# A hybrid encoder trunk on one core: one slot pitch, a fused mask with paired blocks in FoX, and another order in the head

## The chip, the cores and the metric

The kernel runs on one core of a Trainium2 chip. The metric is device time in microseconds (us). TensorE (PE) multiplies, VectorE (DVE) and ScalarE (ACT) work elementwise, GpSimd (POOL) does a little, and SyncE (SP) issues the DMAs.

## The reference

Two layers over x (512 tokens, 1024 features), all fp32. Layer 0 mixes by a chunkwise mLSTM, layer 1 by forgetting attention (FoX) with 16 heads of 64; each is followed by a squared-ReLU MLP of width 4096. Each sub-layer normalises x, scales and shifts it by vectors that come from the condition c, and adds its gated output to x.

```python
mod = silu(c) @ ada_w[l] + ada_b[l]
sh1, sc1, g1, sh2, sc2, g2 = split(mod, 6)
h = rms_norm(x) * (1 + sc1) + sh1
x = x + g1 * mixer(h)                 # mLSTM (l = 0) or FoX (l = 1)
h = rms_norm(x) * (1 + sc2) + sh2
x = x + g2 * (square(relu(h @ w1)) @ w2)
# FoX, per head, for s <= t:
logit[t, s] = q_t . k_s / sqrt(64) + F_t - F_s
out = softmax(where(s <= t, logit, -inf)) @ v
```

## The kernel before, in words

Activations lie transposed, features on partitions, as eight tiles of 128x512. To keep fp32 accuracy every large product is done three times with operands split in a high and a low part (`prod3`, lines 296 to 298, and `gemm_b`, lines 361 to 363): hi·lo, lo·hi, hi·hi. A `unit` (line 138) loads 512 KB of weights and splits them: ACT casts the high part `whi`, DVE subtracts the low part `wlo`.

The tiles of activations come from one pool, `gp`. Slots of tag "g" (40 of them) are 516 columns wide, since the mLSTM's v tiles carry two more columns per head (ones in the high part, zeros in the low); in the built program they start 2,080 bytes apart. Slots of the tags "kt" and "qt" (8 each) are 512 columns wide and start 2,048 bytes apart, and so do the halves of the weight tiles. The MLP's hidden tiles `uh`, `ul` lie in "kt" and "qt" for the chunks c = 0 and 2 and in "g" for c = 1 and 3; h lies in "g", the input of the K and V products (`kvh`, `kvl`) in "kt" and "qt".

**The head.** SP loads a first group `u` of conditioning weights (2 MB), then x (2 MB), a unit of w_in and further groups. PE computes the rows of the conditioning for a group (`ada_rows_first`, line 172: four at a time, each on 32 columns of the array), ACT copies them out, PE transposes them (line 158), and DVE makes shift and scale from them (lines 178 to 181). The mean square of x (squares on ACT, line 250, sums on DVE, line 254, a product with ones on PE, line 262) gives 1/rms by Ln and Exp on ACT (264, 265). `modulated` (285, 287, 288) makes h from it, and the q product runs over k with four banks of PSUM, tag "A". The conditioning rows, their transposes and the mean square share the one bank of tag "C". Then follow the gates and the key product, which takes "A" again, and the v product, "A" too.

**FoX** (from line 565) runs over 8 pairs of heads and 4 query blocks. In a step PE computes the logits of the step after next (686, 687; then `maskb` times `identb` in bf16 adds -1e30 above the diagonal, 688), transposes the probabilities of this step (710), multiplies those of the step before with V (`weighted`, 727), and does two rounds of the q product of a later pair (`FILL`). DVE takes the row maximum (697), ACT the exponential with its row sum (699), DVE the reciprocal and the scaling (700, 701) and half the copies of the transposes (715), ACT the other half (713).

PE, ACT, DVE and SP each take their instructions in order. Where nothing is pinned, a scheduler in the framework places them; in the head the source pins PE's order.

## Time and profile before

| | us |
|---|---|
| median of 3 runs (1242.35 to 1243.93) | 1243.78 |
| the profiled execution's own time | 1243.87 |
| its span | 1241.8 |
| PE busy | 1212.4 (98%) |
| DVE busy | 715.0 (58%) |
| ACT busy | 486.5 (39%) |
| first product of the q projection starts | 27.82 |

A span row gives busy time of matmuls whose ends are modelled and overlap; what a product costs is read from one start to the next. In the timeline a row has start, length, engine, line, operation, output<-inputs, shapes, count, and in brackets the idle time before it and what ended it. In the windows a row has the window, its length, busy us and count of PE, PEld (weight loads), DVE, ACT and POOL, then the granted clock, the DMA engines' share and GB/s. In the groups a row ends with busy us, mean ns of one, and the idle time before.

### The profile page before, as it was taken

The page shows a single profiled execution, that of the slowest core. Times are in us where ns is not written, and L with a number is a line of the kernel's source. Part 1 is how long each engine was busy: PE and PEld are TensorE (multiplying, and loading weights), DVE is VectorE, ACT ScalarE, POOL GpSimd, SP SyncE. Part 2 cuts the span into 40 slices and gives each one's busy share as a digit, 9 for nine tenths or more (in the row PEclk, how much of TensorE's full clock was granted, in tenths as well). Part 3 has the DMA queues.
Part 4 walks back from the last instruction along what each step waited for, and adds up shares of the span by engine and source line. Part 5 has one row for each costly group of instructions (what it writes and reads, how often), then busy time and mean ns, then how long its engine had stood idle before and what let it go on. Part 6 is the DMA issues. An engine that isn't in the chain of part 4 may idle for free.

```text
span 1241.8 us, 16417 instructions
## 1 busy us (share of the span) xinstructions
PE 1212.4 (98%) x6262; PEld 990.3 (80%) x6262; DVE 715.0 (58%) x1193; ACT 486.5 (39%) x876; POOL 56.9 (5%) x78
## 2 busy tenths in 40 slices
PE   4999999999999999999999999999999999999997
PEld 1677888897887888788988877779988888888886
DVE  3687568797656664575565467764843443333344
ACT  3443664264123233133445456643632332332343
POOL 0001001100000000000100111101000000000001
PEclk9999999999999999999999999999999999999999
DMA  9666215546644663565143354422332323323312
GB/s 337 237 206 194 86 51 178 177 138 203 216 158 144 205 193 102 169 209 165 35 122 99 116 144 104 111 58 68 106 105 95 102 88 99 97 91 102 91 46 68
DMA packets 66255, 165.01 MB, mean 133 GB/s; under 512 B 9537, under 2 KB 11841, under 8 KB 66177
## 3 DMA queue, kind: packets, MB, share of 16 engines
q1 hardware_dynamic: 65088, 162.92, 42.1%
q8 instruction: 49, 0.80, 0.3%
q10 hardware_dynamic: 1088, 1.05, 0.3%
q14 instruction: 30, 0.24, 0.1%
HBM read 153.39 MB, written 2.10 MB: 125 GB/s over the span
## 4 chain that ended last, share of the span: by engine, by line
PE 91%; DVE 4%; DMA 3%; ACT 1%; issue 1%; SPq 0%; DVEq 0%; ACTq 0%
PE ga L296 22%; PE ga L298 22%; PE ga L297 22%; PE gb L361 4%; PE gb L363 3%; PE gb L362 3%; DMA araw<-in_adaw_dram 2%; PE oT L727 2%; PE q L651 2%; PE pT L710 1%; PE q L652 1%; PE q L653 1%; PE lg L686 1%; DVE wlo L138 1%; PE lg L687 1%; PE ada L172 1%
## 5 line engine op out<-in xcount | busy, mean ns | idle before, releaser
L138 DVE TENSOR_TENSOR wlo<-raw,whi 128x1024 fp32r<-128x1024 f32 x192 | 236.3, 1231 | 270.0 <-ACT whi L137 268.7
L137 ACT CAST whi<-raw 128x1024 fp32r<-128x1024 f32 x192 | 201.1, 1049 | 454.5 <-PE ga L298 367.0
L296 PE MATMUL ga<-hl,whi 128*128 128x512 f32 (+1 forms) x640 | 238.7, 373 | 1.0 <-DVE hl L288 1.0
L298 PE MATMUL ga<-hh,whi 128*128 128x512 f32 (+1 forms) x640 | 238.0, 372 | 0.0
L297 PE MATMUL ga<-hh,wlo 128*128 128x512 f32 (+1 forms) x640 | 237.8, 372 | 0.0
L296 PE MATMUL ga<-ul,whi 128*128 128x512 f32 (+1 forms) x576 | 211.6, 367 | 0.0
L297 PE MATMUL ga<-uh,wlo 128*128 128x512 f32 (+1 forms) x576 | 211.4, 367 | 0.0
L298 PE MATMUL ga<-uh,whi 128*128 128x512 f32 (+1 forms) x576 | 211.3, 367 | 0.0
L202 DVE SCALAR_TENSOR_TENSOR adaacc<-araw,cond,adaacc 128x512 f32<-128x512 f32 x140 | 106.0, 757 | 73.6 <-DMA araw<-in_adaw_dram 72.2
L296 PEld LDWEIGHTS ga<-hl,whi 128*128 128x128 f32 x640 | 120.5, 188 | 28.6 <-DVE hl L288 3.9
L298 PEld LDWEIGHTS ga<-hh,whi 128*128 128x128 f32 x640 | 120.4, 188 | 22.4
L297 PEld LDWEIGHTS ga<-hh,wlo 128*128 128x128 f32 x640 | 120.4, 188 | 22.4
L296 PEld LDWEIGHTS ga<-ul,whi 128*128 128x128 f32 x576 | 108.3, 188 | 19.5 <-issue 0.8
L298 PEld LDWEIGHTS ga<-uh,whi 128*128 128x128 f32 x576 | 108.2, 188 | 19.3 <-issue 0.8
L297 PEld LDWEIGHTS ga<-uh,wlo 128*128 128x128 f32 x576 | 108.3, 188 | 18.5
L784 DVE SCALAR_TENSOR_TENSOR x<-ga,mod,x 128x512 f32<-128x512 f32 (+1 forms) x72 | 46.0, 688 | 29.4 <-PE ga L298 29.4
L770 DVE TENSOR_TENSOR r<-r 128x512 f32<-128x512 f32 (+1 forms) x72 | 44.2, 626 | 17.8 <-ACT r L769 17.8
L254 POOL TENSOR_TENSOR sq<-sq,sq 128x512 f32<-128x512 f32 x12 | 17.8, 1481 | 790.7 <-ACT sq L250 790.3
L769 ACT ACTIVATE r<-ga 128x512 f32<-128x512 f32 (+1 forms) x72 | 38.6, 547 | 38.3 <-PE ga L298 37.7
L361 PE MATMUL gb<-wlo,hh 128*128 128x512 f32 x128 | 51.1, 401 | 0.8 <-DVE kl L138 0.8
L362 PE MATMUL gb<-whi,hl 128*128 128x512 f32 x128 | 50.6, 396 | 0.0
L363 PE MATMUL gb<-whi,hh 128*128 128x512 f32 x128 | 50.4, 395 | 0.0
(199 smaller groups left out, 1695.2 us busy)
## 6 DMA issues: line engine op xcount, KB each, us to landing
raw<-in_w_dram SPq DMA_DIRECT2D x128, 512.0 KB, 3.6
araw<-in_adaw_dram SPq DMA_DIRECT2D x160, 256.0 KB, 3.4
raw<-in_win_dram SPq DMA_DIRECT2D x24, 512.0 KB, 4.0
u<-in_adaw_dram SPq DMA_DIRECT2D x32, 256.0 KB, 5.9
raw<-in_wkv_dram SPq DMA_DIRECT2D x16, 512.0 KB, 3.6
raw<-in_woa_dram SPq DMA_DIRECT2D x8, 512.0 KB, 3.5
raw<-in_wq_dram SPq DMA_DIRECT2D x8, 512.0 KB, 3.6
q<-qh SPq DMA_DIRECT2D x32, 128.0 KB, 2.3
```

The source lines that it names most:

```text
L137: nc.scalar.copy(dst_hi, src)
L138: dve.tensor_tensor(dst_lo, src, dst_hi.bitcast(F32), op=ALU.subtract)
L202: stt(acc[g], u, cond[:, k:k + 1], acc[g], op0=ALU.mult, op1=ALU.add)
L296: put(mm(ps[:, sl], wh[:, kk, c], rlo[k][:, sl], start=k == 0, stop=False))
L297: put(mm(ps[:, sl], wl[:, kk, c], rhi[k][:, sl], start=False, stop=False))
L298: put(mm(ps[:, sl], wh[:, kk, c], rhi[k][:, sl], start=False, stop=k == NJ - 1))
L361: mm(ps[t], lhi[k][:, c], wl[:, kk], start=k == 0, stop=False)
L362: mm(ps[t], llo[k][:, c], wh[:, kk], start=False, stop=False)
L363: mm(ps[t], lhi[k][:, c], wh[:, kk], start=False, stop=k == NJ - 1)
L769: act(r, ps[:, sl], AF.Relu)
L770: dve.tensor_tensor(r, r, r, op=ALU.mult)
L784: stt(xt[j][:, sl], ps[:, sl], modc(l, G2, j), xt[j][:, sl], op0=ALU.mult, op1=ALU.add)
```

## The change

**Pitch.** All slots of `gp` are 512 columns wide. The high parts of v get a pool of their own (`vp`, four tiles of 516), the low parts lose their two columns of zeros (the product with them writes 256 columns instead of 258). A pad of 128 bytes stands ahead of `gp`; in the built program every slot of `gp` then starts at the same place modulo 2,048 bytes, and as far from the weight tiles, modulo 2,048, as "kt" and "qt" did before. "g" has 37 slots instead of 40.

**FoX.** q and its bias row are negated, so the logits come out negated. The bf16 mask product goes; a DVE instruction adds a mask (0 or 1e30) to the logits out of PSUM, writes the sum to SBUF and its row minimum beside it; ACT takes the exponential from SBUF. The transposes of two query blocks are put side by side, and `weighted` runs once for two query blocks, with 256 columns where both need the key block.

**Head.** x is loaded first, then the unit of w_in, then the first conditioning group in two halves of 128 columns each for shift and scale. The mean square stands first on PE. The second conditioning group's rows come after the q products of k = 0 and 1. Twelve products of the key projection (k = 0, 1; m = 0, 1, banks "B") are done between the conditioning groups, and the key projection uses "BBAA".

```diff
-GSLOT = 2 * (DV + 2)
+VW = 2 * (DV + 2)
...
-    gp = ctx.enter_context(tc.tile_pool(name="gp", bufs=40))
+    vp = ctx.enter_context(tc.tile_pool(name="vp", bufs=NT))
+    pad = ctx.enter_context(tc.tile_pool(name="pad", bufs=1))
+    gp = ctx.enter_context(tc.tile_pool(name="gp", bufs=37))
+    pad.tile([P, 32], F32, name="pad")
...
-                mm(ps[:, ts], identb, maskb, start=False, stop=True)
...
-                dve.tensor_reduce(mx, ps[:, :n], axis=AX.X, op=ALU.max, negate=True)
-                act(p, ps[:, :n], AF.Exp, bias=mx, accum_out=dn)
+                dve.tensor_tensor_reduce(p, LG[a, i][:, :n], mask[:, S - n:], 1.0, POS, ALU.add, ALU.min, mx)
+                act(p, p, AF.Exp, bias=mx, scale=-1.0, accum_out=dn)
...
+                for jp, t in enumerate(PT[pr, i // 2, a]):
+                    js = slice(2 * jp, min(2 * jp + 2, i + 1))
+                    src = tp[:, js.start * P:js.stop * P].rearrange("p (j q) -> p j q", q=P)
...
+                    mm(oT[64 * a:64 * a + 64, (i - 1) * P + q0:(i + 1) * P], V[j, h // 8][:, c:c + DH], PT[pr, i // 2, a][j // 2][:, j % 2, q0:],
...
-            if n:
+            if n and not i % 2:
                 weighted(*steps[n - 1])
...
+    uq = [unit(win[0, 0])]
+    u = ada_load(0, HALF)
+    r0 = rstd(FULL, [squares(range(6), FULL), squares((6, 7), FULL)], put=pin)
+    rows = [ada_rows_first(u[0])]
+    ada_first(0, rows[0])
+    modulated(0, SH1, 0, r0, FULL, hhi, hlo, js=(0,))
+    rows = ada_rows_first(u[1])
+    ada_first(1, rows)
+    modulated(0, SH1, 0, r0, FULL, hhi, hlo, js=(1,))
+    u, = ada_load(1)
+    qproj0(0)
+    qproj0(1)
+    kpre = {"us": [unit(win[1, 0])], "ps": {m: bank("ga", "B") for m in range(2)}, "k": 2}
```

The order of PE at the program's start, before: `ada` are conditioning rows, `adaT` their transposes, `ms` the mean square, `ga` the q product.

```order
L172 MATMUL ada_164<-u_143,condb_98 32x512
...
L158 MATMUL adaT_175<-ident,adarow_173 128x128 x4
L262 MATMUL ms_206<-sq_184,ones_d 128x512
L262 MATMUL ms_206<-sq_204,ones_d 128x512
L172 MATMUL ada_246<-u_233,condb_98 32x512
...
L172 MATMUL ada_246<-u_236,condb_98 32x512
L296 MATMUL ga_212<-hl_132,whi_219 128x512
```

PE at the same place, now (lines 268, 174, 183 and 302 are the old 262, 172, 158 and 296):

```order
L268 MATMUL ms_200<-sq_178,ones_d 128x512
L268 MATMUL ms_200<-sq_195,ones_d 128x512
L174 MATMUL ada_210<-u_157,condb_105 32x256
...
L183 MATMUL adaT_221<-ident,adarow_219 128x128 x2
L174 MATMUL ada_232<-u_157,condb_105 32x256
...
L183 MATMUL adaT_243<-ident,adarow_241 128x128 x2
L302 MATMUL ga_206<-hl_132,whi_151 128x512
```

The mean square has moved to the front, the first group's rows stand in two halves, and the second group's rows (`ada_246` before) are behind the products of k = 0 and 1.

PE where the key product (`ga_557`, `ga_558`) ends and the v product (`gb`) starts, before:

```order
L298 MATMUL ga_557<-hh_131,whi_671 128x512
L296 MATMUL ga_558<-hl_139,whi_671 128x512
L297 MATMUL ga_558<-hh_131,wlo_670 128x512
L298 MATMUL ga_558<-hh_131,whi_671 128x512
L361 MATMUL gb_720<-wlo_726,hh_124 128x512
```

And now, with the first key products (`ga_300`, `ga_301`) right behind the second conditioning group (`ada_302`):

```order
L174 MATMUL ada_302<-u_260,condb_105 32x512
L302 MATMUL ga_300<-hl_132,whi_297 128x512
...
L302 MATMUL ga_301<-hl_132,whi_297 128x512
...
L183 MATMUL adaT_319<-ident,adarow_311 128x128 x4
L302 MATMUL ga_300<-hl_133,whi_297 128x512
...
L304 MATMUL ga_600<-hh_131,whi_689 128x512
L367 MATMUL gb_738<-wlo_744,hh_124 128x512
```

The last key products now fill the two "A" banks that were taken last, and `gb_738` starts in one that the key product did not use.

PE in one step of FoX, from the logits `lg` of block 1 on (`pT` transposes, `oT` V products), before:

```order
L686 MATMUL lg_6830<-k_1317_6612,q_1332_6670 128x256
L687 MATMUL lg_6830<-k_1179_6118,q_1183_6122 128x256
L688 LDWEIGHTS identb
L688 MATMUL lg_6830<-maskb,identb 128x128
L686 MATMUL lg_6834<-k_1334_6678,q_1333_6674 128x256
L687 MATMUL lg_6834<-k_1180_6119,q_1184_6123 128x256
...
L710 MATMUL pT_6852<-ident,p_6791 128x128 x4
L710 MATMUL pT_6859<-ident,p_6798 128x128 x4
L727 MATMUL oT_6771<-pt_6806,V_5540 64x128
L727 MATMUL oT_6771<-pt_6812,V_5540 64x128
```

And now, about the logits of the same size:

```order
L739 MATMUL oT_6994<-pt_6893,V_5556 64x256
...
L739 MATMUL oT_6994<-pt_6897,V_5558 64x128
L695 MATMUL lg_7011<-k_1379_6807,q_1392_6857 128x256
L696 MATMUL lg_7011<-k_1182_6137,q_1186_6141 128x256
L660 MATMUL q_6917<-hl_5807,whi_6914 128x512
L661 MATMUL q_6917<-hh_5799,wlo_6913 128x512
L695 MATMUL lg_7014<-k_1394_6865,q_1393_6861 128x256
L696 MATMUL lg_7014<-k_1183_6138,q_1187_6142 128x256
...
L718 MATMUL pT_7031<-ident,p_6966 128x128 x4
```

The mask's product and weight load are gone, V products come for two blocks at once, and the scheduler has put products of the q projection between the logits of the two heads.

DVE in the same stretch, now (705 is the new instruction; its second row reads out the row minimum):

```order
L705 ISA p_7077,mx_7075<-lg_7011,mask_5788 128x256
L705 ISA mx_7075 128x1
L728 COPY pt_7091<-pT_7089 128x128
L705 ISA p_7084,mx_7082<-lg_7014,mask_5788 128x256
...
L136 TENSOR_TENSOR wlo_7703<-raw_7701,whi_7704 128x1024
L707 RECIPROCAL dn_7076<-dn_7076 128x1
```

Each of the 64 row minima is thus two instructions, where there was one, and DVE's queue holds 82 instructions more in all (1,275 for 1,193).

## Rows read from the trace of the kernel before

**Rows 1.** The page's part 4: the chain that ended last, by engine.

```profile
...
PE 91%; DVE 4%; DMA 3%; ACT 1%; issue 1%; SPq 0%; DVEq 0%; ACTq 0%
...
```

**Rows 2.** Waits of PE (what waited for what: us in total, times, longest).

```profile
...
PE ga L296 <- DVE hl L288: 1.0, 1, 1.0
...
PE gb L361 <- DVE kl L138: 0.8, 1, 0.8
...
```

**Rows 3.** Timeline of the head: start, us, engine, line, operation, tiles, shapes, [idle].

```profile
10.55 1.94 PE L172 MATMUL ada<-u,condb 128*32 128x512 f32 x8 [1.00 <-DMA u<-in_adaw_dram]
...
11.87 5.65 SPq L164 DMA_DIRECT2D u<-in_adaw_dram  x8
...
13.12 4.26 ACT L250 ACTIVATE sq<-x 128x512 f32<-128x512 f32 x8
...
19.65 3.75 PE L262 MATMUL ms<-sq,ones_d 128*128 128x512 f32 x4 [5.20 <-DVE sq L254]
...
23.51 0.69 ACT L264 ACTIVATE rstd<-ms,eps 128x512 f32<-128x512 f32 x1 [5.19 <-PE ms L262]
...
24.25 3.64 PE L172 MATMUL ada<-u,condb 128*32 128x512 f32 x16 [0.84 <-ACT rstd L264]
...
26.43 0.75 DVE L288 SCALAR_TENSOR_TENSOR hl<-w,mod,hh 128x512 fp32r<-128x512 f32 x1 [0.79 <-ACT hh L287]
...
27.82 0.80 PE L296 MATMUL ga<-hl,whi 128*128 128x512 f32 x1
...
34.58 1.92 PE L172 MATMUL ada<-u,condb 128*32 128x512 f32 x16
...
```

**Rows 4.** Three MLP stages of layer 1: window, us, busy (count) by engine.

```profile
921.19:964.48 43.29, 43.29 (x192) 35.85 (x191) 17.93 (x22) 10.95 (x14) 0.00 (x0) 1.00 0.30 95
964.71:1008.93 44.22, 44.22 (x193) 35.87 (x192) 16.53 (x19) 13.57 (x18) 0.00 (x0) 1.00 0.30 94
1009.16:1053.54 44.38, 44.38 (x192) 35.85 (x191) 18.67 (x22) 11.55 (x15) 0.00 (x0) 1.00 0.30 94
```

**Rows 5.** Groups by shape: line, op, tiles, shape, count | busy us, mean ns.

```profile
...
L297 PE MATMUL ga<-hh,wlo 128*128 128x512 f32 x512 | 201.7, 394 | 0.0
...
L297 PE MATMUL ga<-uh,wlo 128*128 128x512 f32 x448 | 175.3, 391 | 0.0
...
```

**Rows 6.** One head pair of the attention loop, columns as in group 4.

```profile
778.56:793.10 14.54, 14.54 (x110) 11.19 (x110) 11.47 (x32) 9.21 (x25) 2.56 (x2) 1.00 0.45 113
```

**Rows 7.** PE's timeline in that pair.

```profile
783.03 1.09 PE L727 MATMUL oT<-pt,V 128*64 128x128 f32 x16
...
784.06 0.50 PE L651 MATMUL q<-hl,whi 128*128 128x512 f32 x1
...
785.56 0.39 PE L686 MATMUL lg<-k,q 128*128 128x512 f32 x1
...
785.79 0.40 PE L687 MATMUL lg<-k,q 128*128 128x512 f32 x1
...
786.06 0.48 PE L686 MATMUL lg<-k,q 128*128 128x512 f32 x1
...
786.68 0.61 PE L710 MATMUL pT<-ident,p 128*128 128x128 f32 x4
...
787.22 0.44 PE L727 MATMUL oT<-pt,V 128*64 128x128 f32 x4
...
787.59 0.50 PE L651 MATMUL q<-hl,whi 128*128 128x512 f32 x1
...
```

**Rows 8.** Groups by shape in 740 to 836 us, DVE and ACT.

```profile
...
L699 ACT ACTIVATION_READ_ACCUMULATOR p<-lg,mx 128x1 f32 x52 | 10.2, 197 | 0.0
...
L697 DVE TENSOR_REDUCE mx<-lg 128x1 f32<-128x512 f32 x14 | 9.5, 679 | 0.0
...
L700 DVE RECIPROCAL dn<-dn 128x1 f32<-128x1 f32 x52 | 7.5, 155 | 6.4 <-ACT p L699 5.8
...
L657 DVE SCALAR_TENSOR_TENSOR ql<-q,qh 128x512 fp32r<-128x512 f32 x5 | 3.4, 681 | 0.0
...
```

More of the change, by code (lines that the diff above doesn't have):

```diff
@@ L10 @@
 F32R = mybir.dt.float32r
-BF16 = mybir.dt.bfloat16
 AF = mybir.ActivationFunctionType
@@ L72, in slot @@
         if tag == "g":
-            return gp.tile([P, GSLOT], dt, name=nm(name), tag="g")[:, :n]
+            return gp.tile([P, S], dt, name=nm(name), tag="g")[:, :n]
         return gp.tile([P, S], dt, name=nm(name), tag=tag, bufs=8)[:, :n]
@@ L153, in ada_rows, with ada_cols, ada_load @@
         return rows
-    def ada_cols(rows, n=P, put=lambda i: i):
+    def ada_cols(rows, n=P):
         tp = bank("adaT", "C")
         for b in range(4):
-            put(nc.tensor.transpose(tp[:, b * n:(b + 1) * n], rows[:, b * P:(b + 1) * P], ident[0:n, 0:n]))
+            nc.tensor.transpose(tp[:, b * n:(b + 1) * n], rows[:, b * P:(b + 1) * P], ident[0:n, 0:n])
         return tp
-    def ada_load(q):
+    def ada_load(q, parts=(FULL,)):
         u = [slot(name="u", tag=("kt", "qt")[q % 2]) for _ in range(NJ)]
-        for k in range(NJ):
-            nc.sync.dma_start(u[k], adaw0[q, k // 2, :, k % 2 * S:k % 2 * S + S])
-        return u
+        for c in parts:
+            for k in range(NJ):
+                o = k % 2 * S
+                nc.sync.dma_start(u[k][:, c], adaw0[q, k // 2, :, o + c.start:o + c.stop])
+        return [[u[k][:, c] for k in range(NJ)] for c in parts]
     def ada_rows_first(u):
+        n = u[0].shape[1]
         ps = bank("ada", "C")
@@ L171, in ada_rows_first, with ada_first @@
             c = 32 * (k % 4)
-            pin(mm(ps[c:c + 32, :], condb[:, k, :], u[k], start=k < 4, stop=k >= 4))
-        return ada_rows(ps)
-    def ada_first(q, rows):
-        tp = ada_cols(rows, put=pin)
-        t = small(4, "adat")
-        dve.tensor_reduce(t, tp.rearrange("p (b c) -> p b c", c=P)[:, :, 0:P:32], axis=AX.X, op=ALU.add)
-        j = 2 * q
-        dve.tensor_tensor(mod[0][:, j:j + 2], t[:, 0:2], colv(C_ADAB + j, 2), op=ALU.add)
-        stt(omsc[0][:, j:j + 2], t[:, 2:4], 1.0, colv(C_ADAB + 8 + j, 2), op0=ALU.add, op1=ALU.add)
+            pin(mm(ps[c:c + 32, :n], condb[:, k, :], u[k], start=k < 4, stop=k >= 4))
+        rows = slot(name="adarow", n=n)
+        nc.scalar.copy(rows, ps[:, :n])
+        return rows
+    def ada_first(j, rows):
+        nj = rows.shape[1] // 256
+        tp = bank("adaT", "C")
+        for b in range(2 * nj):
+            pin(nc.tensor.transpose(tp[:, b * P:(b + 1) * P], rows[:, b * P:(b + 1) * P], ident))
+        t = small(2 * nj, "adat")
+        dve.tensor_reduce(t, tp[:, :2 * nj * P].rearrange("p (b c) -> p b c", c=P)[:, :, 0:P:32], axis=AX.X, op=ALU.add)
+        dve.tensor_tensor(mod[0][:, j:j + nj], t[:, 0::2], colv(C_ADAB + j, nj), op=ALU.add)
+        stt(omsc[0][:, j:j + nj], t[:, 1::2], 1.0, colv(C_ADAB + 8 + j, nj), op0=ALU.add, op1=ALU.add)
     fill = []
@@ L310, in gemm_a @@
         held[0] = tg
-        ps = [pre["ps"] if pre and m == 0 else bank("ga", tg[m]) for m in range(4)]
+        ps = [pre["ps"][m] if pre and m in pre["ps"] else bank("ga", tg[m]) for m in range(4)]
         for k in range(NJ):
@@ L317, in gemm_a @@
             for m in range(4):
-                if not (pre and m == 0 and k < pre["k"]):
+                if not (pre and m in pre["ps"] and k < pre["k"]):
                     step(ps[m], k, m, sl)
@@ L412, in out_proj, with mlstm @@
                 squares_low()
-    def mlstm(l, hhi, hlo, G0, qps, between):
+    def mlstm(l, hhi, hlo, G0, qps, kpre, between):
         qh, ql, kh, kl = [], [], [], []
@@ L454, in mlstm @@
         nc.scalar.copy(gc.rearrange("p t c -> p (t c)"), tp[:, :NT * 64])
-        gemm_a([win[1, i] for i in range(4)], hhi, hlo, ev_k, tag="AAAA")
+        gemm_a([win[1, i] for i in range(4)], hhi, hlo, ev_k, tag="BBAA", pre=kpre)
         rate[0] = RATES[1]
@@ L599, in fox @@
         split(Gh[0:16], Gl[0:16], G)
+        mask = slot(name="mask")
+        nc.gpsimd.memset(mask, 0.0)
+        nc.gpsimd.affine_select(mask[:, S - P:], mask[:, S - P:], pattern=[[-1, P]], compare_op=ALU.is_ge, fill=POS, base=0, channel_multiplier=1)
         oh, ol = [None] * NJ, [None] * NJ
@@ L832, in tile_encoder @@
     t, half = norm2(0)
-    mlstm(0, hhi, hlo, G0, qps, lambda: half(0))
+    mlstm(0, hhi, hlo, G0, qps, kpre, lambda: half(0))
     rate[0] = RATES[3]
```

92 lines of the change are left out of this document (46 added, 46 removed).

## The prediction, made before the changed kernel was timed

> **What bounds the kernel now.** I read the chain that ended last first: 91% of it is PE [rows 1]. So an edit is worth what it takes off PE's queue or off a stall of PE. Next the waits of PE and the timeline of the head: beside two short stalls later [rows 2] nearly all idle time of PE lies before 27.82 us, where the first product of the q projection starts [rows 3]. Then, since PE is full after that, the windows of single stages, to see what a product costs where nothing waits: three MLP stages of 192 products each take 43.29, 44.22 and 44.38 us from the first start to the last [rows 4]. Last the attention loop by pair of heads: PE full for 14.54 us, DVE busy 11.47 of them [rows 6]. The profiled execution took 1243.87 us, its span of 1241.8 and 2.07 around it; it stands 0.1 us from the median of the runs shown, so the sum is made against 1243.9.
>
> **1. One pitch.** The three stages of [rows 4] run the same three lines on the same shapes; PE's clock reads 1.00 in all, the weight loads take 35.85 to 35.87 us, and DVE and ACT are half idle. They differ in where the moving operand lies: "qt" and "kt" slots (`ul`, `uh` of chunk 0) in the first, h in "g" slots in the second, `uh` of chunk 1 in "g" slots in the third. Over 191 steps that is 226.7, 231.5 and 232.4 ns a product. The same code with chunk 0 and with chunk 1 differs by 5.7 ns, so I put it down to the slots. After the change all slots lie as the fast ones did, towards each other and towards the weights. Products of 512 columns that move out of "g" slots: h 3 x 512 (the x512 of [rows 5], once for each line of a product), and of `uh`, `ul` chunks 1 and 3: by the loops, 3 x 192 of the 3 x 448 [rows 5]; besides 288 of the q and the out projection in FoX. 1536 + 288 = 1824 products are 9.5 stages of 0.93 us (44.22 - 43.29) = 8.8 us; 576 are 3 stages of 1.09 = 3.3 us. 384 products of `gb` have h as the stationary operand; no row here prices that alone, so between 0 and 2 stages of 0.93, and I take 1.0. Products of 256 columns I count at 0. Sum: -13.1 us; bounds -9 (only half of the h products gain) to -14.
>
> The trace cannot tell pitch from address by itself. The Trainium skill ("SBUF — State Buffer", Specifications) states 16-byte cachelines as the only granularity; both pitches and all starts are multiples of that, so by the rule nothing would be gained here, and the sum would be short by all of this term. The 5.7 ns between two chunks of one code speak against it.
>
> Three slots fewer in "g" I cost at 0: four v tiles have left it, and so have the transposed probabilities of FoX (they go to "araw" and "acc" slots, idle there). If it runs out, a DVE or ACT write waits for a release.
>
> **2. Head.** DMAs first. The eighth 256 KB tile of SP's queue is seen at 10.55, where PE waits for it [rows 3]; x is now these first eight. Later ones come at 5.65/8 = 0.7 us per 256 KB [rows 3]. The last square ends 4.26/8 = 0.53 us after 10.55, its sum (one DVE addition, about 0.65) at 11.8; the product with ones takes 3.75 for two [rows 3], the first of which now runs before that, so it ends at 13.75; Ln frees bank "C" 0.8 later (23.51 + 0.69 against 19.65 + 3.75), at 14.55. The unit of w_in (0.5 MB) and the first half group (1 MB) have landed by 10.55 + 6 x 0.7 = 14.75. Half a group of rows at the slow level takes 3.64/2 = 1.8 [rows 3]: 16.55. A copy, two transposes and a small DVE reduction (0.16 by [rows 8]) I estimate at 1.2, so the bank is free at 17.8; the second half ends at 19.6, its copy and transposes at 20.7. h takes 2.3 from the scales on (before, 3.0 from the end of Ln, 24.20, to the end of `hl`, 27.18, less an Exp as long as Ln [rows 3]): 18.1 + 2.3 = 20.4. First q product: 20.7 instead of 27.82, 7.1 us earlier.
>
> Given back: the second group's rows stood before 27.82 and now stand behind; 1.92 + 0.1 at the fast level [rows 3], so +2.0. PE's clock: the same 16 records took 3.64 at 24.25 and 1.92 at 34.58, its levels of 1.2 and 2.4 GHz; before, the stream started at the slow level and left it after three products (the first is busy 0.80 [rows 3]). PE now comes out of a head with more gaps; I take 7 products at half pace (512 columns are 0.43 us at 1.2 GHz, for 0.23), 1.5 instead of 0.6 us, so +0.9. The twelve key products are work moved, not removed; they cover the chain from a group's transposes to h. With them and with the free banks the waits for `hl` (1.0) and for `kl` (0.8) [rows 2] go, -1.8. Every DMA that is moved past others still lands ahead of its use: the second group by 10.55 + 18 x 0.7 = 23.2, wanted at 27. SP issues 16 small DMAs where it issued 8; at 0.7 us or less each they keep the queue fed. Sum: -7.1 + 2.0 + 0.9 - 1.8 = -6.0. Bounds: -2 (the clock slow for 10 us, a stall of 1 us stays) to -9 (no clock loss, no stall at the gates).
>
> **3. FoX on PE.** Logits of 512 columns: from 785.56 to 786.68 are four products and two masks in 1.12 us; a plain product steps by 0.23 (785.56 to 785.79) [rows 7], so without masks 0.92: 0.20 a step. The first head's share is 0.50, 0.04 over its two products; the second's, behind the first mask, is 0.62 [rows 7]. At 32 steps that is 6.4 us at most; in blocks of 128 and 256 columns the weight loads should pace the products anyway, and I take -5.0, bounds -2.6 (64 x 0.04) to -6.4. V products: 16 records from 783.03 to 784.06, four from 787.22 to 787.59 [rows 7]: 0.22 per 128 columns and 0.15 per group. Ten column blocks in four groups become ten in two: -0.3 a pair, -2.4 in all; bounds 0 to -3. Together -7.4.
>
> **4. FoX on DVE.** The new instruction reads PSUM and SBUF, writes 512 columns and a minimum. The trace has no such instruction. Nearest: the row maximum, 679 ns at 512, and a two-operand instruction out of PSUM, 681 [rows 8]; I take 0 extra for it. The read-out of the minimum is new: ACT's costs up to 197 ns, a one-column DVE instruction 155 [rows 8], half hidden behind its neighbours; 0.1 x 8 a pair. Two copies more a pair, 0.3. DVE goes from 11.47 to 12.6 us a pair while PE falls from 14.54 to 13.5 (0.9 from part 3, 0.12 of pitch). DVE at 93%, in order, with waits for ACT in it, will hold PE at times: about 0.3 us a pair, +2.4. Bounds 0 to +6 (read-out at its full 197 and the present waits kept). Net FoX: -5.0.
>
> The negation of q costs nothing (the same scaled copies). The mask is made on POOL while it is idle. 40 products of 256 instead of 258 columns: under 0.1 us.
>
> **Sum:** 1243.9 - 13.1 - 6.0 - 5.0 = 1219.8.
>
> **Rivals.** (a) *The pitch gives nothing*, because the 5 ns come from what DVE and ACT write beside it, or from addresses that differ again. For it: only one pair of chunks shows it so cleanly, and a rule says so. Against: the second and the third stage agree though their neighbours differ. Time: 1243.9 - 11 = 1233. (b) *DVE becomes FoX's bound*, the new instruction running at half the rate of the row maximum. Mean width 320 columns, mean row maximum about 0.48 us, of which some 0.33 goes with the columns; 0.33 more in 8 of a pair is +2.7, DVE 15.3 against PE's 13.5. FoX then costs 8 x (15.3 - 14.54) = +6 instead of -5: 1231. For it: nothing in the trace prices the instruction. (c) *Slower*: the same place, the instruction nearly three times as long as the row maximum. DVE decides from 13.5 - 12.6 = 0.9 us a pair, 0.11 each; each further 0.1 costs 64 x 0.1 = 6.4 us. Without stalls the gain is 13.1 + 6.0 + 7.4 = 26.5; to eat it the instruction must be 0.11 + 26.5/64 = 0.52 us longer, more than double its mean length; at 0.8 it costs 44 us: 1261. Against it: no DVE row of this width is near that. (d) *The head's gain is spent*: waits move to the gates' chain or the conditioning rows, and the 6 us become 1: 1225; it is within the forecast's spread.
>
> **How the numbers follow.** Forecast, all three parts with (d) in it: 0.74, its own range 1212 to 1229. (a) 0.11, (b) 0.11, (c) 0.04. Range 1212 to 1233 takes in (a) and (b)'s likelier halves and leaves out about 0.15. No change means within 0.2%, 2.5 us. Faster 0.94 (all but 0.02 of the first three cases); same 0.02, between (b) and (c); slower 0.04.
>
> **What would show it.** Pitch: all MLP stages of 192 products at about 43.3 us; if h's stage stays at 44.2, part 1 is wrong. Head: first q product near 20.7, the last key product followed by the v product without a wait. FoX: 13.5 to 13.9 us a pair; the new instruction near 0.68 at 512 columns; if PE's idle time names DVE there and the pair takes 14.5 or more, (b). I am wrong above 1233 or below 1212, and in the reasons if one part gives twice its term and another none.

## The result, and the profile after

| | before | after |
|---|---|---|
| time, median of the runs | 1243.07 us (1242.1 to 1243.93) | 1232.26 us (1231.01 to 1233.31) |
| ratio | 1 | 0.9909, 95% interval 0.9897 to 0.9921 |
| span of the profiled execution | 1241.8 us | 1230.0 us |

The change is worth 11 us where 24 were forecast. The span splits at starts of products that both traces have (us; the sum is the difference of the spans):

| from ... to | before | after | difference |
|---|---|---|---|
| start to the first product of mLSTM's values | 86.71 | 79.46 | -7.25 |
| to the MLP's first product in layer 0 ("the mLSTM stretch") | 169.82 | 172.75 | +2.93 |
| MLP of layer 0, to the first product of V | 363.58 | 358.71 | -4.87 |
| V and K | 91.16 | 91.17 | +0.01 |
| FoX, from the first q product behind K to the last V product | 122.88 | 126.19 | +3.31 |
| output projection | 41.41 | 39.73 | -1.68 |
| MLP of layer 1 to the end | 366.19 | 361.97 | -4.22 |

Head and MLPs did about what was forecast; the mLSTM stretch and FoX, where the forecast had gains, became longer.

The three MLP stages after (windows; us, then busy and count of PE, PEld, DVE, ACT, POOL, the granted clock, DMA's share, GB/s):

```profile
913.53:956.82 43.29, 43.29 (x192) 35.86 (x191) 17.98 (x22) 10.99 (x14) 0.00 (x0) 1.00 0.30 96
957.05:1000.34 43.29, 43.29 (x192) 35.86 (x191) 16.53 (x19) 13.57 (x18) 0.00 (x0) 1.00 0.31 95
1000.57:1043.86 43.29, 43.29 (x192) 35.86 (x191) 18.59 (x22) 11.62 (x15) 0.00 (x0) 1.00 0.30 96
```

Against [rows 4] all three now have the time that only the first had.

The head after, PE's timeline (start, us, line, operation, tiles, shapes, what ended the idle time before):

```profile
15.32 1.07 PE L174 MATMUL ada<-u,condb 128*32 128x256 f32 x16 [0.84 <-ACT rstd L270]
...
17.71 2.22 PE L174 MATMUL ada<-u,condb 128*32 128x256 f32 x16 [0.26 <-DVE adat L185]
...
20.85 0.78 PE L302 MATMUL ga<-hl,whi 128*128 128x512 f32 x1
...
21.85 0.63 PE L304 MATMUL ga<-hh,whi 128*128 128x512 f32 x1
22.27 0.63 PE L302 MATMUL ga<-hl,whi 128*128 128x512 f32 x1
...
24.77 0.40 PE L302 MATMUL ga<-hl,whi 128*128 128x512 f32 x1
25.01 0.39 PE L303 MATMUL ga<-hh,wlo 128*128 128x512 f32 x1
```

The first product of q starts at 20.85 instead of 27.82 [rows 3]. Up to 24.4 the products step by 0.43 us (21.85 to 22.27), PE's lower level, and from 24.77 on by 0.24 or less.

FoX as one window, before, after, and with one line changed (the first experiment), in this order:

```profile
711.27:834.15 122.88, 122.88 (x884) 93.86 (x883) 90.33 (x248) 73.46 (x199) 16.62 (x13) 1.00 0.43 109
```

```profile
702.08:828.27 126.19, 117.89 (x699) 89.97 (x698) 90.66 (x328) 77.68 (x215) 16.66 (x13) 0.99 0.41 106
```

```profile
701.68:816.58 114.90, 112.25 (x695) 88.64 (x694) 93.11 (x328) 76.18 (x215) 16.76 (x13) 1.00 0.46 117
```

PE was busy all the time before. After, its busy time is 5 us less and it stands still for 8.3 (126.19 less 117.89). DVE is busy for 91 of 126 us: it isn't full. What DVE and PE waited for in that window (us in total, times, longest), of after:

```profile
DVE pt L728 <- PE pT L718: 8.7, 13, 1.5
DVE p L705 <- POOL k L644: 4.4, 3, 2.1
...
DVE ol L136 <- POOL k L644: 2.1, 1, 2.1
```

```profile
PE lg L695 <- DVE mx L705: 3.1, 3, 1.5
PE pT L718 <- DVE p L708: 2.1, 4, 1.0
PE pT L718 <- DVE dn L707: 1.5, 3, 0.6
PE lg L695 <- DMA k<-k: 1.5, 1, 1.5
```

L705 is the combined instruction, L644 POOL's subtraction that makes k2. One such place in the timeline of after:

```profile
748.09 2.62 POOL L644 TENSOR_TENSOR k<-kf,k 64x512 fp32r<-64x512 f32 x2 [12.79 <-PE lg L696]
...
749.42 0.40 PE L662 MATMUL q<-hh,whi 128*128 128x512 f32 x1
...
750.74 0.56 DVE L705 CUSTOM_DVE_ANT_0 p<-lg,mask 128x384 f32<-128x384 f32 x1 [2.07 <-POOL k L644]
...
751.34 0.62 ACT L706 ACTIVATE p<-p,mx 128x384 f32<-128x384 f32 x1 [2.35 <-DVE mx L705]
...
751.36 0.33 PE L695 MATMUL lg<-k,q 128*128 128x128 f32 x1 [1.54 <-DVE mx L705]
```

The logits stand ready, DVE is idle for 2.07 us and starts 0.03 us after POOL is done; then ACT follows, and PE, which needs the logits' bank, starts a product 1.94 us after it started the last one. The program's own list of waits says why. It has on DVE, in the change, and on ACT, before:

```
806 L705 ISA p_1358_6734,mx_1356_6732<-lg_1336_6673,mask_1109_5788 128x384 [waits Pool_49]
479 L699 ACTIVATE p_1251_6374,dn_1250_6372<-lg_1232_6319,mx_1249_6371 128x512 [waits DVE_49,Pool_49]
```

`p_1358` lies in the buffer that `kf_1178` had, and the two subtractions that read `kf_1178` are those at 748.09. The row max of before wrote one column and needed no buffer; its wait for one fell to the exponential on ACT, behind it, where the trace of before shows no time lost to POOL. The combined instruction writes the block itself, so DVE waits, in order, one step earlier.

### The profile page after: what moved, and what is told of

It reads as the page before. It is cut to its first block, busy times and chain, and to the rows that moved or that the text cites. A ratio compares the mean times of both kernels' runs of the same rounds, so it can differ in the third digit from the quotient of the medians.

```text
span 1230.0 us, 16175 instructions
## 1 busy us (share of the span) xinstructions
PE 1193.8 (97%) x6086; PEld 988.5 (80%) x6086; DVE 713.7 (58%) x1275; ACT 491.8 (40%) x893; POOL 54.7 (4%) x70
## 4 chain that ended last, share of the span: by engine, by line
PE 81%; DVE 3%; DMA 2%; issue 1%; ACT 1%; POOL 1%; SPq 0%; DVEq 0%; POOLq 0%; ACTq 0%
PE ga L302 22%; PE ga L303 22%; PE ga L304 22%; PE gb L367 2%; PE gb L369 2%; PE gb L368 2%; PE oT L739 2%; DMA araw<-in_adaw_dram 2%; PE pT L718 1%; PE q L660 1%; PE q L662 1%; PE q L661 1%; POOL k L644 1%; DVE adaacc L208 1%; PE lg L695 1%
## 5 line engine op out<-in xcount | busy, mean ns | idle before, releaser
L208 DVE SCALAR_TENSOR_TENSOR adaacc<-araw,cond,adaacc 128x512 f32<-128x512 f32 x140 | 106.0, 757 | 86.7 <-DMA araw<-in_adaw_dram 85.7
L303 PEld LDWEIGHTS ga<-uh,wlo 128*128 128x128 f32 x576 | 108.6, 189 | 17.5
L135 ACT CAST uh<-r 128x512 fp32r<-128x512 f32 (+1 forms) x72 | 40.8, 573 | 29.7 <-DVE r L782 29.4
```

The lines of the kernel that those rows point to most:

```text
L135: nc.scalar.copy(dst_hi, src)
L208: stt(acc[g], u, cond[:, k:k + 1], acc[g], op0=ALU.mult, op1=ALU.add)
L303: put(mm(ps[:, sl], wl[:, kk, c], rhi[k][:, sl], start=False, stop=False))
```

## The experiments

"FoX", "mLSTM stretch" and "MLPs" are the stretches of the table. Two runs of the same mLSTM instructions (the pitch alone, with and without own buffers for p in FoX) gave 173.3 and 170.3 there, so a single profile tells nothing under some 3 us in that stretch (half of the difference is the granted clock, 0.97 from the last value product to the MLP in the one and 1.00 in the other). In FoX and the MLPs runs of the same instructions agree within 0.8, but for the clock (below). Ratios are to runs of the kernel before on the same chip.

| kernel | time, us | ratio to before (95%) | mLSTM | FoX | MLPs |
|---|---|---|---|---|---|
| after, p in own buffers | 1221.93 | 0.9823 (0.981 to 0.9835) | 171.7 | 114.9 | 359.0, 362.0 |
| ... and old softmax, paired | 1226.27 | 0.9851 (0.9835 to 0.9867) | 172.1 | 117.5 | 359.5, 362.0 |
| ... and combined, unpaired | 1227.08 | 0.9864 (0.9847 to 0.988) | 173.5 | 119.3 | 358.7, 362.0 |
| pitch alone, p in own buffers | 1234.30 | 0.9922 (0.9907 to 0.9937) | 170.3 | 122.1 | 358.9, 362.0 |
| pitch alone | 1239.14 | 0.9962 (0.995 to 0.9974) | 173.3 | 126.5 | 358.7, 362.0 |
| after, old softmax, paired | 1231.01 | 0.9898 (0.9886 to 0.9911) | 171.9 | 125.4 | 359.2, 362.1 |
| old pitch, pool split 36 + 4 | 1265.66 | 1.0177 (1.0162 to 1.0192) | 173.5 | 134.6 | 367.0, 369.3 |
| after, no pad | 1252.02 | 1.0073 (1.0059 to 1.0087) | 174.2 | 129.4 | 367.1, 368.8 |
| after, one step back | 1236.56 | 0.9948 (0.9935 to 0.9961) | 174.4 | 129.1 | 359.1, 362.0 |

**Own buffers for the wide blocks of p.**

```diff
-                p = temp(name="p")[:, :n] if n <= 256 else slot(name="p", n=n)
+                p = temp(name="p")[:, :n] if n <= 256 else vp.tile([P, VW], F32, name=nm("p"), tag="v")[:, :n]
```

> The changed kernel, with the probabilities of the 384 and 512 wide blocks written into the four buffers that held v's upper parts (idle in the FoX stage) instead of buffers of the shared pool g. Nothing else is moved. Theory S (buffer): the new combined instruction on DVE writes a whole block, so it must wait until the last reader of that block's old content is done, among them POOL's k2 subtraction (2.6 us for two); before, the row max had no such output and the wait fell on ACT's exponential, which had room. Under S the idle times before the combined instruction that are put down to POOL (4.4 us in three waits) and most of PE's gaps go: the FoX stage, 126.4 us in the changed kernel and 123.1 before, takes 118 to 121.5, the kernel 1224 to 1228. Theory L (shared use of SBUF): the combined instruction, which reads PSUM and SBUF, can't run while POOL's subtraction runs, whichever buffer it writes: FoX stays at 126 +-1, the kernel at 1232. Theory D (DVE's sheer load and the order on PE): 124 to 126, the kernel 1230 to 1232.

FoX falls to 114.9, below the expected 118 to 121.5, and the kernel to 1221.9: theory S (the buffer), with more in it than was thought. DVE's waits in FoX are now (the view of DVE's waits from above, of this kernel):

```profile
DVE p L705 <- PE lg L696: 6.4, 14, 2.2
...
DVE ol L136 <- POOL k L644: 1.5, 1, 1.5
```

The combined instruction waits for logits alone. Theory L fails by this run's own timeline, where it starts and ends inside a subtraction of POOL's at its usual duration (after's mean at 512 is 679 ns):

```profile
747.50 1.30 POOL L644 TENSOR_TENSOR k<-kf,k 64x512 fp32r<-64x512 f32 x1
747.90 0.68 DVE L705 CUSTOM_DVE_ANT_0 p<-lg,mask 128x512 f32<-128x512 f32 x1
```

**The two halves of FoX, each undone, with own buffers.** Mask product, row max and exponential from PSUM put back; or the blocks unpaired as before; or neither part there (the pitch alone with the edit above). The first also has `mm(ps[:, ts], identb, maskb, ...)` behind the logits and q not negated, the second `transposed` and `weighted` of the kernel before:

```diff
-                dve.tensor_tensor_reduce(p, LG[a, i][:, :n], mask[:, S - n:], 1.0, POS, ALU.add, ALU.min, mx)
-                act(p, p, AF.Exp, bias=mx, scale=-1.0, accum_out=dn)
+                dve.tensor_reduce(mx, LG[a, i][:, :n], axis=AX.X, op=ALU.max, negate=True)
+                act(p, LG[a, i][:, :n], AF.Exp, bias=mx, accum_out=dn)
```

```diff
-            if n and not i % 2:
+            if n:
                 weighted(*steps[n - 1])
```

> The changed kernel with mask product, row max and exponential as before, paired blocks kept, and the wide probabilities in the four idle buffers of v. It stands against the same with the combined instruction (FoX, from the first query product after the last conditioning of K to the last V product, 114.9 us, kernel 1221.9). Theory S2 (once the buffers are there, PE's work is what FoX costs): the 64 mask products come back at about 5 us: FoX 118.5 to 121, the kernel 1225.5 to 1228. Rival T2 (the buffers did it all and the combined instruction is worth nothing, since DVE bounds FoX either way): FoX 114 to 116.5, the kernel 1221 to 1223.5.

> The changed kernel with the blocks unpaired as before (a transposed block in a buffer of pool g, each V product 128 wide), the combined instruction kept, and the wide probabilities in the four idle buffers of v. Theory S2 (PE's work decides once the buffers are there): the V products cost the 2.4 us of the forecast again, and the transposed blocks use pool g again: FoX 117 to 120 against 114.9, the kernel 1224 to 1227. Rival T2 (pairing costs as much on DVE and ACT, in copies, as it saves on PE): FoX 113.5 to 115.5, the kernel 1220 to 1222.5. Rival T3 (it is the transposed blocks' buffers that matter, which pairing takes out of pool g): FoX 122 or more, the kernel 1229 or more.

> The pitch alone on the kernel before, and the wide probabilities in the four idle buffers of v; FoX's instructions are those of the kernel before. The pitch alone had FoX at 126.5 us against 122.9 before, the kernel at 1239.1. Theory S (three buffers fewer in pool g is what FoX paid): with four given back FoX takes 119 to 123.5, no longer than before, and the kernel 1232 to 1236. Rival U (v's own pool, the new pitch or the order on PE is what FoX paid): FoX stays at 125.5 or more, the kernel at 1238 to 1240.

The four make a square: neither 122.1, combined alone 119.3, paired alone 117.5, both 114.9. The combined instruction is worth 2.9 without pairing and 2.6 with it, pairing 4.6 and 4.4: they add. With the old softmax FoX came out a little under its theory (117.5 for 118.5 to 121), with unpaired blocks inside it. Theory S holds in the kernel before too: with the pitch alone FoX takes 126.5, with own buffers 122.1.

**The pitch alone; the old softmax without own buffers.** The first is the kernel before with pool, v buffers and product order of the change (its diff, without head and FoX, but with the 12 small buffers, `sm`, that the change has for 16); the second is the changed kernel with the first half of the diff above.

> The kernel before with the pitch alone: pool g at 2,048 bytes with 37 buffers, v's upper parts in a pool of their own, v's lower parts 512 wide, the pad and 12 small buffers. Theory P: the pitch alone is worth the two MLP stretches, -4.9 and -5.9 us in the comparison of the two traces, and one or two us in the attention stages: 1230 to 1232.5 us, all MLP groups of 192 products at 43.3 us, FoX 121.5 to 123.5 (123.1 before), output projection of mLSTM to the MLP's first product 39 to 40 us. Rival Q: three buffers fewer cost stalls; FoX 124 to 127 or the output projection 42 to 44 us, the kernel 1233 to 1237. Rival R: the pitch does nothing, and the MLP gain comes from the other parts: 1242 us.

> The changed kernel with the mask put back as a product on PE, the row max as a reduction on DVE and the exponential read from PSUM; the paired blocks, the pitch and the new head stay. Theory S: the stalls of the combined instruction go (about 8 to 10 us of PE gaps) and the 64 mask products come back (5 us on PE by the forecast): FoX 120.5 to 124 against 126.4, the kernel 1226 to 1230. Rival T (the stalls come from the paired blocks, their extra copies and the new order of products on PE): FoX 127 to 132, the kernel 1233 to 1238.

The pitch alone gives the MLPs all of their gain (-4.9 and -4.2) and the kernel 4 us: what is missing sits in FoX (+3.6) and in the mLSTM stretch (+3.5), as rival Q had it, and more. With the old softmax FoX takes 125.4, 0.8 less than in the change and between the two theories: the mask products are there, and so is the lack of buffers, for which its exponential waits on ACT. ACT's waits in FoX, of the pitch alone and then of the old softmax:

```profile
ACT p L701 <- POOL k L637: 4.6, 3, 1.7
```

```profile
ACT p L710 <- POOL k L647: 4.6, 3, 1.7
```

The kernel before and the kernels with own buffers have no such wait on ACT or DVE; the change has it on DVE (4.4). How much of it reaches PE differs. With own buffers PE stands still 5.7 us less under the combined instruction (8.3 to 2.7), 2.8 less under the old softmax with paired blocks (3.3 to 0.6) and 2.3 less without pairing (2.3 to 0). The 125.4 also hold two stretches at a lower granted clock (0.79 from 750.82 to 758.82 and from 766.82 to 774.82), the change one, the old softmax with own buffers none, so the whole times 125.4, 126.2 and 117.5 don't compare by the softmax and the buffers alone.

**The old pitch with the split pool.**

```diff
-    gp = ctx.enter_context(tc.tile_pool(name="gp", bufs=40))
-    sm = ctx.enter_context(tc.tile_pool(name="sm", bufs=16))
+    gp = ctx.enter_context(tc.tile_pool(name="gp", bufs=36))
+    sm = ctx.enter_context(tc.tile_pool(name="sm", bufs=12))
+    vp = ctx.enter_context(tc.tile_pool(name="vp", bufs=NT))
...
-                a = slot(F32R, GSLOT, name="vh").rearrange("p (h d) -> p h d", h=2)
+                a = vp.tile([P, GSLOT], F32R, name=nm("vh"), tag="v").rearrange("p (h d) -> p h d", h=2)
```

> The kernel before with its old pitch of 2,064 bytes, but the pool split as in the change: 36 buffers in pool g and four of v's upper parts in a pool of their own (40 in all, as before), and 12 small buffers. Nothing else. Theory S: the split alone costs the mLSTM stage's end and FoX: from mLSTM's last set of value products to the MLP 62 to 64 us against 58.8 before, FoX 125.5 to 128 against 122.9; the MLP stretches stay at 363.6 and 366.2; the kernel 1248 to 1253. Rival V (faster products under the new pitch run into DVE and the DMAs, and that is what the two stages paid): both stages stay within 1 us of before and the kernel at 1242 to 1244.

FoX becomes longer, as theory S says, and more than it expected (134.6, the kernel 1265.7), but the MLPs, which neither theory moved, became 3 us longer each. So this run changes buffers and the time of a product at once, and its FoX doesn't price the buffers alone. The stage with `uh`, `ul` in "kt" and "qt" buffers, whose pitch is 2,048 bytes in every kernel here, is the first below; [rows 4] has it at 43.29:

```profile
939.93:984.50 44.57, 44.57 (x193) 35.85 (x192) 18.14 (x22) 10.99 (x14) 0.00 (x0) 1.00 0.29 94
984.72:1029.11 44.39, 44.39 (x192) 35.88 (x191) 16.54 (x19) 13.56 (x18) 0.00 (x0) 1.00 0.29 94
```

Four buffers fewer in pool g had moved those of "kt" and "qt" by 8,320 bytes (four times 2,080; the expectation's 2,064 is the width of a slot, not its pitch). Their distance to the first tile of the weights' upper parts, by the program's allocation, was 103,680 bytes, a multiple of 256; it became 95,360, 128 bytes off one.

**No pad.**

```diff
-    pad = ctx.enter_context(tc.tile_pool(name="pad", bufs=1))
...
-    pad.tile([P, 32], F32, name="pad")
```

> The changed kernel without its pad of 128 bytes ahead of pool g, so that all of the pool's buffers move down by 128 bytes against the weight tiles; their pitch stays 2,048. Theory P1 (the even pitch is what made the products fast): products of 512 columns stay at 226.6 ns, the MLP stretches at 358.7 and 362.0 us, the kernel at 1230 to 1233. Rival P2 (what counts is where the moving buffer lies against the weight tile, and the even pitch only puts all buffers at the same place): in the run with the old pitch and the split pool the buffers of K and Q, whose pitch was 2,048 there as well, lay 128 bytes off the place they have here and before, and their products took 233 ns. Under P2 all products of the MLPs take 231 to 234 ns, each MLP stretch is 8 to 12 us longer, and the kernel takes 1250 to 1262.

```profile
929.53:973.91 44.38, 44.38 (x192) 35.98 (x191) 18.05 (x22) 10.91 (x14) 0.00 (x0) 1.00 0.31 94
974.14:1018.54 44.40, 44.40 (x193) 35.99 (x191) 16.54 (x19) 13.58 (x18) 0.00 (x0) 1.00 0.29 92
1018.77:1063.15 44.38, 44.38 (x193) 35.98 (x191) 18.72 (x22) 11.56 (x15) 0.00 (x0) 1.00 0.31 95
```

The kernel is 20 us slower: 8.4 and 6.9 in the MLPs and 2.2 in V and K are the 128 bytes. The 3.2 in FoX are not: the run one step back, further down, has the same 129 there with the pad in place, through falls of the granted clock.

The pitch is even here and the MLPs' products take 232.4 ns: rival P2. An even pitch only makes all buffers alike; the pad puts them where a product takes 226.6 ns. Which power of two counts isn't settled: the four places tried (226.6 ns a product at two places 1,280 bytes over a multiple of 2,048, 232.4 and 233.4 at two places 1,152 over one) fit more than one.

In the trace of before, steps of products from those "g" slots that lie a multiple of 256 from the weights (177 by the program's allocation) took 231.0 ns, within the 229.5 to 233.3 of slots at other places: either a larger power of two counts, or the neighbours of a buffer do. Nor is the distance to the weights told from the buffers' own address: in before, after and the two runs that moved the buffers the weight tiles start at the same place modulo 512.

**One conditioning step back, and what lengthens mLSTM.** The changed program loads K's first unit before the list of conditioning steps exists, so one step fewer was taken with it.

```diff
+    tick()
     mlstm(0, hhi, hlo, G0, qps, kpre, lambda: half(0))
```

> The changed kernel, with one conditioning step taken from the list right ahead of the mLSTM stage. Theory M1: K's first weight unit is now loaded before the list of conditioning steps exists, so one step fewer is issued with K's units, and the list runs one step late from there on: in the output projection DVE waits for a conditioning weight's DMA in front of the instruction that PE waits for (PE gaps of 1.70 us at 200.2 and 3.32 us at 240.1, against none and 1.68 before). With the step given back, the stretch from the first output projection product of the second group to the MLP's first product takes 39.8 to 41 us instead of 43.8, and the kernel 1228 to 1230. Theory M2 (fewer buffers in the pool, or the earlier start itself, makes the gaps): the stretch stays at 43 to 44 us, the kernel at 1232.

M1 fell: the stretch didn't get shorter, and the kernel is 4 us slower than the change. 2.9 of them are in FoX, whose products stand in the same order as in after. The same stall lies, in the two kernels, at the start of these windows (columns as above, the clock third from the end), of this run and then of after:

```profile
736.00:744.00 8.00, 6.33 (x32) 4.31 (x31) 4.75 (x21) 3.79 (x13) 1.26 (x1) 0.79 0.36 101
...
752.00:760.00 8.00, 6.17 (x30) 3.95 (x29) 5.45 (x24) 4.09 (x14) 1.98 (x2) 0.80 0.37 99
```

```profile
734.00:742.00 8.00, 6.28 (x41) 4.81 (x40) 5.93 (x27) 4.89 (x17) 1.26 (x1) 1.00 0.32 93
```

After 1.65 us between the starts of two products (1.38 of them idle) the granted clock fell here and not there, and twice 1.4 to 1.5 us more went, beside the stall itself. Another fall is in both kernels (0.79 from 766.08 to 774.08 in after). The run without the pad has all three, and there FoX keeps step with this run to 0.3 us.

In the mLSTM stretch DVE waits, from the last value product to the MLP, for conditioning weights; of before, of after:

```profile
DVE adaacc L202 <- DMA araw<-in_adaw_dram: 7.0, 7, 3.1
DVE adaacc L200 <- DMA araw<-in_adaw_dram: 1.4, 2, 0.8
```

```profile
DVE adaacc L208 <- DMA araw<-in_adaw_dram: 8.9, 10, 2.6
DVE adaacc L206 <- DMA araw<-in_adaw_dram: 3.4, 2, 2.9
```

8.4 us before, 12.3 after. One of them, in DVE's timeline of after, holds the low part of y, for which PE waits 1.32 us until 201.93:

```profile
200.40 0.75 DVE L208 SCALAR_TENSOR_TENSOR adaacc<-araw,cond,adaacc 128x512 f32<-128x512 f32 x1 [1.62 <-DMA araw<-in_adaw_dram]
...
201.15 0.72 DVE L558 SCALAR_TENSOR_TENSOR yl<-yT,col,yh 128x512 fp32r<-128x512 f32 x1
```

Five kernels tell such waits from the other suspects. Four are made from "after, p in own buffers", one from the kernel before.

The steps ahead (and 1.5 and 0.5 in place of 2.0 and 0.0):

```diff
-RATES = (1.0, 1.0, 1.0, 2.8, 1.05)
+RATES = (1.0, 2.0, 0.0, 2.8, 1.05)
```

Output products early (`early(i)` issues `prod3` for k = 2i, 2i + 1 and all four m of `woa[0]`, into four "A" banks):

```diff
         mix(2)
+        early(0)
         mix(3)
+        for i in range(1, 2):
+            early(i)
         ytrans(2)
```

No loads, on the changed kernel and on the one before:

```diff
-                u = wrp.tile([P, S], F32, name=nm("araw"), tag="araw", bufs=2)
-                nc.sync.dma_start(u, adaw[q // 4, q % 4, kp, :, kk * S:kk * S + S])
+                if g == 0 and k < 2:
+                    st[kk] = wrp.tile([P, S], F32, name=nm("araw"), tag="araw", bufs=2)
+                    nc.sync.dma_start(st[kk], adaw[q // 4, q % 4, kp, :, kk * S:kk * S + S])
+                u = st[kk]
```

> The changed kernel with the wide probabilities in v's idle buffers, and the conditioning steps run at two per weight unit in the value and gate products of mLSTM and at none per unit in its output projection, so that DVE waits for no conditioning weight there. Theory A (the conditioning steps in DVE's order are what lengthened the end of mLSTM): from the last value product to the MLP's first product 58 to 60.5 us, against 62.6 with the steps in the stretch and 59.0 before; the kernel 1217.5 to 1220. Theory B (the order on PE is: 39 products of the numerator in a row behind the values, where the kernel before had 18 and then output projection products): 62 to 64 us, the kernel 1221 to 1224. A price is possible under both: more conditioning work beside the values, up to 2 us.

> The changed kernel with the wide probabilities in v's idle buffers, and the first 16 sets of three products of mLSTM's output projection (the heads that are done) issued between and behind the numerators of the last two heads, in four banks that are idle there. The conditioning steps stay where they are. Theory B (order on PE): PE's gaps of 0.7, 1.0 and 1.2 us between the numerators and ahead of the transposes are filled: 58.5 to 60.5 us from the last value product to the MLP's first product, the kernel 1217.5 to 1220. Theory A (DVE's waits for conditioning weights, which hold the chain whatever PE does): the stretch stays at 62 to 64 us, the kernel at 1221 to 1223.5, and the gap ahead of the norm's product grows by what was filled.

> The changed kernel with the wide probabilities in v's idle buffers, and of each set of conditioning vectors only the first two weight blocks loaded; the other steps work on those again, so DVE has the same instructions but no transfer to wait for (the loads of the other conditioning weights are left out, so the conditioning is not the reference's). Theory A1 (what holds DVE in mLSTM is the wait for a conditioning weight's transfer in front of instructions that PE needs): from the first value product to the MLP's first product 166 to 169 us against 171.7 with the loads and 169.8 before, most of it in the end (from the last value product 58 to 60 us against 62.6); the kernel 1216 to 1219. Theory A2 (it is the conditioning work itself on DVE, 1.5 us a step): the stretch stays at 170.5 to 172.5, the kernel at 1220 to 1223.

> The kernel before with the same loads left out. Theory A1 (the faster products of the change meet the conditioning weights' transfers, which did not get faster; before there was slack for them): little to gain here, 168.5 to 170 us from the first value product to the MLP's first product against 169.8, the kernel 1240 to 1243.5. Rival A3 (the waits were there before as well, and the change's loss in mLSTM is something else): 165 to 168 us, as much less as in the changed kernel, the kernel 1237 to 1240.

> The changed kernel with the wide probabilities in v's idle buffers, and conditioning steps at 1.5 per weight unit beside mLSTM's values and at 0.5 in its output projection (1 and 1 in the change, 2 and 0 in the run with the steps put ahead, which won 6.3 us at the end of mLSTM and paid 5.2 of it back beside the values). Theory A: with fewer steps put ahead less is paid back: from the first value product to the MLP's first 167 to 170 us, the kernel 1217 to 1219.5. Rival: what is won at the end is paid in front at any rate: 170.5 to 172, the kernel 1219.5 to 1222.

| kernel | time, us | ratio (95%) | first to last value product | to the MLP | sum |
|---|---|---|---|---|---|
| before | 1243.07 | 1 | 110.8 | 59.0 | 169.8 |
| after, p in own buffers | 1221.93 | 0.9823 | 109.0 | 62.6 | 171.7 |
| steps ahead | 1219.66 | 0.9815 (0.9802 to 0.9827) | 114.3 | 56.3 | 170.6 |
| 1.5 and 0.5 | 1220.94 | 0.9819 (0.9806 to 0.9833) | 113.1 | 57.7 | 170.8 |
| output products early | 1223.21 | 0.9839 (0.9825 to 0.9854) | 109.2 | 62.3 | 171.4 |
| no loads | 1215.12 | 0.9771 (0.9757 to 0.9784) | 108.8 | 57.4 | 166.3 |
| before, no loads | 1239.68 | 0.9967 (0.9955 to 0.998) | 110.6 | 58.1 | 168.7 |

Without the loads the stretch is 5.4 us shorter in the changed kernel (outside the 3 of two equal runs) and 1.2 in the kernel before: theory A1. The interval of the changed kernel's time doesn't meet that of the same kernel with loads. The kernel before, at 1239.7, came out in rival A3's range; but 3.6 us of its gain are in the head, where kernels with the same head differ by 2.7 (84.0 to 86.7). The stretch from the last value product to the MLP tells more than such sums, since it shows for how long PE stood still (windows as above, of before, after, own buffers, and own buffers without the loads):

```profile
197.53:256.53 59.00, 57.43 (x376) 50.99 (x375) 46.56 (x91) 22.98 (x58) 6.37 (x7) 1.00 0.52 168
```

```profile
188.33:252.21 63.88, 58.96 (x377) 52.08 (x375) 47.58 (x93) 22.67 (x57) 5.80 (x5) 0.97 0.53 168
```

```profile
188.90:251.54 62.64, 58.13 (x377) 50.91 (x376) 47.29 (x92) 22.76 (x57) 5.74 (x5) 1.00 0.54 172
```

```profile
189.02:246.46 57.44, 57.18 (x377) 50.96 (x376) 49.23 (x101) 23.19 (x58) 5.73 (x5) 1.00 0.25 81
```

PE stands still for 1.6 us before, 4.9 after, 4.5 with own buffers and 0.3 without the loads (0.3 too in the kernel before without them). The change adds 3.4 us of standing still here, and in its profile another 1.5 of busy time at a mean granted clock of 0.97. That the loads hold PE longer now because the products in front got faster and the transfers didn't is argued, not shown.

It isn't the work on DVE, which stayed, and not the order on PE alone: products put into its gaps changed nothing in the stretch (62.3; the MLP behind it took 3 us more, with its products in another order, which was not looked into). A proviso: without loads the scheduler also puts PE's products of the stretch in another order in places, so the 5.4 are transfers and that order together. With the steps ahead, 6.3 us go from the end and 5.2 come back in front; at 1.5 and 0.5 it is the same bargain, as the rival had it.

The fastest version with nothing left out is the change with own buffers for p (1221.93) or the same with the steps ahead (1219.66); their intervals overlap. Both beat before and after.

## Why the prediction was wrong in its sum

Of the 12 us that are missing in the span, 8.3 are FoX (+3.3 for -5.0); the rest is the mLSTM stretch, where gains were counted and 2.9 were lost. The time still lies inside the stated range, at its upper end, which was kept for rivals (a) and (b). Neither came about, so that is luck.

- **Pitch, -13.1.** Where a stage has no other limit it is as forecast: 43.29 for 192 products, -4.9 and -4.2 in the MLPs. The -1.7 of the output projection is not the pitch's: with the pitch alone it took 41.3 and 41.8 for 41.4 before. The rest was to come in the head, in the mLSTM stretch and in FoX and can't be seen there. The reason given was half of it: that all slots lie the same "towards each other and towards the weights". Lying the same is not enough (no pad: even pitch, 44.4 everywhere); the place counts, and whether it is the place towards the weights is open. The Trainium skill ("SBUF — State Buffer", Specifications) names cachelines of 16 bytes. By that rule 0 was to be gained; it doesn't cover what was measured, since a move by 128 bytes, eight such lines, cost 17.5 us in the MLPs and in V and K.
- **Head, -6.0.** First q product forecast at 20.7, measured 20.85 here, and between 21.4 and 22.9 in the other profiles with the new head, so the agreement is in part luck. The wait for `kl` is gone, one for `hl` of 0.4 is left, eight or nine products run at half pace where seven were assumed. At the first value product -7.25; but that point lies at 83.1 to 86.7 in the profiles with the old head and at 79.4 to 80.7 in those with the new one, 5 us apart in the mean.
- **FoX on PE, -7.4.** With buffers enough -7.2 (122.1 to 114.9), and 13.1 to 14.2 us a pair from one pair's first 512-wide logits to the next's (the last two, with less of the q product in them, 11.3 and 11.6), around the 13.5 to 13.9 forecast. The shares were off: pairing about 4.5 where 2.4 stood, the mask 2.6 to 2.9 net of DVE's additions.
- **FoX on DVE, +2.4.** The instruction was priced right. Of after, the groups by shape (columns as in [rows 8]):

```profile
L705 DVE CUSTOM_DVE_ANT_0 p<-lg,mask 128x512 f32<-128x512 f32 x16 | 10.9, 679 | 0.7 <-PE pT L718 0.5 <-POOL k L644 0.3
...
L705 DVE CUSTOM_DVE_ANT_0 p<-lg,mask 128x384 f32<-128x384 f32 x16 | 8.6, 549 | 4.1 <-POOL k L644 4.1
```

  679 ns at 512 is the row max of [rows 8], and its read-out takes 0.08 us. Rival (b) had the right time for the wrong reason: no half rate, and DVE not full.
- **The step that failed** is the sentence that costs three slots fewer in "g" at 0 because v's and the transposed tiles had left it, with "if it runs out, a DVE or ACT write waits for a release" behind it. The release was the case. With three slots fewer the engine that writes p waits 4.4 to 4.6 us for POOL's subtraction, where before it lost nothing; FoX pays 3.6 for it with the pitch alone, and in the change giving four buffers back takes 11.3 off FoX (126.2 to 114.9). Of the 11.3, 5.7 are PE standing still, twice as much as where ACT writes p; the rest lies in PE's modelled busy time, where one fall of the clock is a part and the remainder wasn't taken apart. The step was costed by counting tiles, with no look at which engine writes p now and what last read the buffer that p gets. The program's list of waits had both.
- **Not seen at all**: the mLSTM stretch, +2.9 (-1.9 up to the last value product, +4.9 behind it, of which 3.4 is PE standing still and 1.5 the clock). The forecast let the head's and the pitch's gains run through it and never asked what else runs there at a pace of its own. Rival (d) came nearest, but looked for the new wait in the gates' chain and the first groups' rows.

## What to carry to other kernels

When operations are merged, ask which engine writes the large output now, and find the last reader of the buffer that it gets: a wait that costs little on one engine can cost more on another, and a few buffers can outweigh the work saved. An even pitch is not a place: after any change of pools compare a stage with no other limit to its best time, since a shift of all buffers shows there at once. A stage made faster ahead of a stream of loads with two buffers may only meet the stream earlier.

## What the hardware showed that was not expected

- Products of 512 columns take 226.6 or 232 to 233 ns by a shift of 128 bytes of the moving buffers (the weights stayed), at a granted clock of 1.00 and with the weight loads at 35.9 to 36.0 us a stage in both.
- A DVE instruction that reads PSUM and SBUF ran beside POOL's subtraction in SBUF in its usual time (0.68 us), in the one such pair of rows shown.
- Behind the same stalls of the same products PE's granted clock fell in one execution (0.79 and 0.80 in windows of 8 us) and stayed at 1.00 in another; a fall cost 1.4 to 1.5 us.
